# S5 branch of a hybrid encoder block: a quad's kernel emitted one quad ahead of its body

## Chip, cores and metric

One NeuronCore of a Trainium2 chip runs the whole block. The metric is the device time of one execution in microseconds, here the median of three runs. TensorE is written PE, VectorE DVE, ScalarE ACT, GpSimd POOL, SyncE (whose queue issues nearly all DMAs) SP.

## What is computed

The block normalises its input, projects it (`w_in`) and sends parts of the projection through three branches, of which S5 is one; a gated feed-forward stage follows. S5 is a bidirectional diagonal state space model on 32 groups of 16 channels. Of each direction the reference computes

```python
bb_re = coef_re[..., None] * b_re - coef_im[..., None] * b_im
bb_im = coef_re[..., None] * b_im + coef_im[..., None] * b_re
ug = u.reshape(bsz, seq, S5_GROUPS, S5_GROUP)
bu_re = jnp.einsum('blgc,gpc->lbgp', ug, bb_re)
bu_im = jnp.einsum('blgc,gpc->lbgp', ug, bb_im)
...
_, _, s_re, s_im = lax.associative_scan(combine, (a_re, a_im, bu_re, bu_im), reverse=reverse, axis=0)
y = jnp.einsum('lbgp,gcp->blgc', s_re, c_re) - jnp.einsum('lbgp,gcp->blgc', s_im, c_im)
```

and then `z = gelu(y + D*u)` and `z * sigmoid(z @ glu_w + glu_b)`. The last is called the GLU below.

## The kernel before, in words

`emit_s5` goes over eight *quads* of four groups each. Time is cut into 128 blocks of 8 steps. For one quad the program has these parts, in the order in which it emits them.

- **The kernel.** The loads of b and c (`braw`, `craw`, L780 and L781), two transposes of c on PE (`tc`, L786), the powers of the state matrix times c on DVE (`cc`, four products at L797 and two sums at L798), the product of coef and b on POOL (`bb`), and from these the local response of a block, `kp` (L819, eight matmuls), which ACT copies into `Kt` and `kb` (L823, L824) and to which DVE adds the skip term (L825, L826). `Kt` is written to DRAM as lines (L828, L829) and comes back as a Toeplitz matrix `D` by eight loads (L832).
- **Weights of the input.** `Bw` (POOL, by `cmul`), transposed on PE (`tt`, L807, two groups of four) and copied by ACT to `BT` (L809). They stand inside the kernel's code, between `bb` and `kp`. The PSUM tiles `tc`, `tt` and `kp` share one tag with two buffers.
- **The body.** The load of `U` (L835), sine and cosine of the phases (L839 to L850; DVE's share is L840, L841, four times L843, L849, L850), the products of weights and input `bu` on PE (L856, two groups of four), their rotation on DVE (L860 to L862), four scans on DVE (L868, L870), the rotation back to `M` (L875 to L877, one half on DVE, the other on POOL), the outputs `yp` on PE (L881 with `cc` and `M`, L883 with `D` and `U`), and a copy `z` by ACT (L885) that goes to DRAM.

A scheduler that simulates the engines sets the order on each engine; the order in which the program emits is one of its inputs. Each engine executes its list in that order. While S5 runs, PE also works on the projection of the remaining columns (`pj`, three lines L144 to L146 of a helper, with weights that ACT casts to `wh` at L135 and POOL subtracts to `wl` at L136). Behind the last quad come the GLU (loads `zf` at L1263, gelu and split `zh`, `zl` at L1264 to L1266, matmuls `gl`) and a branch whose fold (DVE, L299, L301, L306) runs beside the GLU.

Of the kernel before, what the change touches and what calls it, by code (L numbers as in the profile page):

```python
# [7 lines left out]
F32 = mybir.dt.float32  # L8
# [8 lines left out]
P = 128  # L17
# [422 lines left out]
def combine_odd(E, room, inv, g, ce, so, y):  # L440

    V = E.nc.vector
    for i, z in enumerate((so, ce[:, 3::-1])):
        U, W = inv("U"), inv("W")
        for m, bank in enumerate((U, W)):
            for n in range(2):
                transform(E, bank[:, n], [A5T_OFF + 512 * m + 256 * k + P * n for k in range(2)],
                          [(g[k][m][:, i],) for k in range(2)], n == 0, n == 1, True)
        for out, own, other, t in ((z[:, 0:2], U, W, T_NTAN), (z[:, 3:1:-1], W, U, T_TAN)):
            V.tensor_tensor(out=out, in0=own, in1=out, op=ALU.add)  # L450
# [133 lines left out]
def cmul(E, pool, out, a, b, shape, tag, eng=None, conj=False):  # L584

    eng = eng or E.nc.vector
    for k, op in enumerate((ALU.add, ALU.subtract) if conj else (ALU.subtract, ALU.add)):
        t = [pool.tile(shape, F32, tag=f"{tag}{i}", name=f"{tag}{i}") for i in range(2)]
        pairs = ((a[0], b[0]), (a[1], b[1])) if k == 0 else ((a[1], b[0]), (a[0], b[1]))
        for i in range(2):  # L590
            eng.tensor_tensor(out=t[i], in0=pairs[i][0], in1=pairs[i][1], op=ALU.mult)
        eng.tensor_tensor(out=out[k], in0=t[0], in1=t[1], op=op)
# [145 lines left out]
def emit_s5(E, before):  # L738


    nc, d = E.nc, E.d
    V, GP = nc.vector, nc.gpsimd
    f, b = slice(0, 64), slice(64, 128)
    with ExitStack() as ctx:
        op = ctx.enter_context(E.tc.tile_pool(name="s5k", bufs=1, reuse_waits="tile"))
        ps = ctx.enter_context(E.tc.tile_pool(name="s5_ps", bufs=1, space=PSUM, reuse_waits="tile"))
# [5 lines left out]
        with E.tc.tile_pool(name="s5p", bufs=1, reuse_waits="tile") as pp:  # L752
            coef, r8, wh, wl, ec, eb = s5_params(E, op, pp, ps)
            before()
        sp = ctx.enter_context(E.tc.tile_pool(name="s5", bufs=1, reuse_waits="tile"))
# [13 lines left out]
            GP.memset(t, 0.0)  # L769
        T = lambda tag, shape=None, bufs=1: sp.tile(shape or [P, 4, P], F32, tag=tag, name=tag, bufs=bufs)  # L770
        beside = E.dft.tile([P, 4, 4, P], F32, tag="ax", name="beside")
        for q in range(8):
            gs = slice(4 * q, 4 * q + 4)
            B4 = lambda ap, n: ap[:, gs].unsqueeze(2).to_broadcast([P, 4, n])
            braw = [T(f"braw{i}", [P, 4, 16], 2) for i in range(2)]
# [6 lines left out]
            e4 = lambda ap, n, m: ap[:, :, gs].rearrange("p t g -> p g t").unsqueeze(3).to_broadcast([P, 4, n, m])  # L782
            b4 = lambda ap, n, m: ap.unsqueeze(2).to_broadcast([P, 4, n, m])
            pt = ps.tile([P, 2, 64], F32, tag="tt", name="tc", bufs=2)
# [7 lines left out]
            CC = [T(f"cc{i}", [P, 4, 9, 16], 2) for i in range(2)]  # L792
# [5 lines left out]
                V.tensor_tensor(out=CC[k], in0=tmp[0], in1=tmp[1], op=sgn)  # L798
            Bb = [T(f"bb{i}", [P, 4, 16], 2) for i in range(2)]
            cmul(E, sp, Bb, braw, [B4(coef[0], 16), B4(coef[1], 16)], [P, 4, 16], "bt", GP)  # L800
            Bw = [T(f"bw{i}", [P, 4, 8, 16]) for i in range(2)]
            cmul(E, sp, Bw, [b4(x, 8, 16) for x in Bb], [e4(x, 8, 16) for x in eb], [P, 4, 8, 16], "wt", GP)
            BT = []
            for i in range(2):
                pt = ps.tile([P, 4, P], F32, tag="tt", name="tt", bufs=2)
                for g in range(4):
                    nc.tensor.transpose(pt[:, g], Bw[i][:, g].rearrange("p t c -> p (t c)"), E.ident)  # L807
                bt = T(f"BT{i}")
                nc.scalar.copy(bt, pt)  # L809
                BT.append(bt)  # L810
            for k in range(2):
                for s in range(2):
                    r = slice(64 * s, 64 * s + 64)
# [16 lines left out]
            D = T("D", bufs=2)  # L830
            for t in range(8):
                nc.sync.dma_start(out=D[16 * t:16 * t + 16],  # L832
                                  in_=E.klines[gs, :, 16 * (7 - t):16 * (7 - t) + P].rearrange("g c x -> c g x"))
            U = T("U", bufs=2)
            nc.sync.dma_start(out=U, in_=E.uS[gs].rearrange("g t c j -> (t c) g j"))  # L835
            J = lambda ap: ap[:, gs].unsqueeze(2).to_broadcast([P, 4, P])
# [16 lines left out]
            for i in range(2):  # L853
                pt = ps.tile([P, 4, P], F32, tag=f"bu{i}", name=f"bu{i}")
                for g in range(4):
                    nc.tensor.matmul(out=pt[:, g], lhsT=BT[i][:, g], rhs=U[:, g], start=True, stop=True)  # L856
                bu.append(pt)
            for i, sgn in ((0, ALU.add), (1, ALU.subtract)):
                p = [T(f"rt{k}") for k in range(2)]
# [5 lines left out]
            n = 4 * W  # L865
            for i in range(2):
                o, r, x = fl(S[i]), fl(rd), fl(xs[i])
# [5 lines left out]
            for i, sgn, eng in ((0, ALU.subtract, V), (1, ALU.add, GP)):  # L873
                p = [beside[:, 2 * (q % 2) + k] if i else T(f"rt{k}") for k in range(2)]
# [4 lines left out]
            for g in range(4):  # L879
                for k in range(2):  # L880
                    nc.tensor.matmul(out=yp[:, g], lhsT=CC[k][:, g, 1:9].rearrange("p i c -> p (i c)"), rhs=M[k][:, g],  # L881
                                     start=k == 0, stop=False)
                nc.tensor.matmul(out=yp[:, g], lhsT=D[:, g], rhs=U[:, g], start=False, stop=True)  # L883
            z = T("z")
# [895 lines left out]
def hybrid_block(tc, d):  # L1780
# [4 lines left out]
    with ExitStack() as top:  # L1785
# [18 lines left out]
        with ExitStack() as s0:  # L1804
            E.h0 = pool(s0, "h0")
            E.dft = pool(s1, "dft")
            with ExitStack() as s2:
# [25 lines left out]
                for ct in range(4):  # L1833
                    emit_conv(E, ct)
                emit_ada(E, (2, 4, 3), *ada_rooms(E))
                emit_s5(E, lambda: [emit_u(E, ct) for ct in range(4)])
                for ct in range(4, 12):
                    emit_conv(E, ct)
# [70 lines left out]
```

## Time and profile before

| | us |
|---|---|
| median of 3 runs (lowest, highest) | 1742.25 (1740.11, 1743.9) |
| the profiled execution | 1741.92 |
| its span | 1740.1 |
| busy in the span: PE, DVE, ACT, POOL | 1548.8, 1352.2, 720.0, 674.4 |
| S5 stretch, from the first quad's `M` to the last's | 430 to 629 |
| GLU matmuls | 674 to 701 |

The span is that of the one core; the time of an execution adds what lies around it (1.8 us here). Busy shares are averages over stages that are bound by different engines, so the S5 stretch is read by itself below. In the rows a time is the start in us from the start of the span, followed by the duration; what stands in brackets is the time that the engine idled before, and what it waited for. A matmul of f32 shows up as two rows of the trace.

### The profile page before, as it was taken

The page shows a single profiled execution, that of the slowest core. Times are in us where ns is not written, and L with a number is a line of the kernel's source. Part 1 is how long each engine was busy: PE and PEld are TensorE (multiplying, and loading weights), DVE is VectorE, ACT ScalarE, POOL GpSimd, SP SyncE. Part 2 cuts the span into 40 slices and gives each one's busy share as a digit, 9 for nine tenths or more (in the row PEclk, how much of TensorE's full clock was granted, in tenths as well). Part 3 has the DMA queues.
Part 4 walks back from the last instruction along what each step waited for, and adds up shares of the span by engine and source line. Part 5 has one row for each costly group of instructions (what it writes and reads, how often), then busy time and mean ns, then how long its engine had stood idle before and what let it go on. Part 6 is the DMA issues. An engine that isn't in the chain of part 4 may idle for free. (4 is left out here: it accounts for less than half of the span.)

```text
span 1740.1 us, 21907 instructions
## 1 busy us (share of the span) xinstructions
PE 1548.8 (89%) x7470; PEld 1282.4 (74%) x7470; DVE 1352.2 (78%) x1945; ACT 720.0 (41%) x1326; POOL 674.4 (39%) x475
## 2 busy tenths in 40 slices
PE   6777889998777798998869999899999999999996
PEld 2666768776666676786757989688888888878884
DVE  6889798688999935788887666976676777579976
ACT  5846455543333325412223355533333333245445
POOL 3356654329775526768862121111111111011242
PEclk9999999998888899999979999899999999999998
DMA  9446643423232235874326753143323223499963
GB/s 330 122 140 185 194 120 111 154 77 102 64 78 58 76 98 168 292 236 146 120 85 208 258 176 97 49 137 112 103 91 103 91 97 103 147 374 312 331 193 124
DMA packets 245318, 263.81 MB, mean 152 GB/s; under 512 B 28120, under 2 KB 169264, under 8 KB 243765
## 3 DMA queue, kind: packets, MB, share of 16 engines
q1 hardware_dynamic: 244726, 259.99, 47.0%
q0 software_dynamic: 480, 2.42, 0.4%
q8 instruction: 59, 0.97, 0.2%
q14 instruction: 53, 0.43, 0.1%
HBM read 195.00 MB, written 67.34 MB: 151 GB/s over the span
## 5 line engine op out<-in xcount | busy, mean ns | idle before, releaser
L144 PE MATMUL pj<-hT,wh 128*128 128x512 f32 x480 | 196.0, 408 | 10.0 <-ACT cva L1180 8.9
L146 PE MATMUL pj<-hT,wl 128*128 128x512 f32 x480 | 194.5, 405 | 3.5 <-POOL wl L136 3.5
L136 POOL TENSOR_TENSOR wl<-wf,wh 128x1024 fp32r<-128x1024 f32 (+1 forms) x56 | 130.5, 2330 | 157.6 <-ACT wh L135 129.8
L136 POOL TENSOR_TENSOR wl<-wg,wh 128x1024 fp32r<-128x1024 f32 x22 | 54.7, 2488 | 346.9 <-ACT wh L135 346.8
L146 PE MATMUL gu<-h2T,op 128*128 128x512 f32 x440 | 173.1, 394 | 4.3 <-DVE op L136 4.3
L144 PE MATMUL gu<-h2T,op 128*128 128x512 f32 x440 | 171.4, 394 | 2.6 <-ACT op L135 2.5
L145 PE MATMUL gu<-h2T,op 128*128 128x512 f32 x440 | 172.7, 392 | 0.0
L135 ACT CAST op<-ws 128x512 fp32r<-128x512 f32 x88 | 54.4, 621 | 181.3 <-PE gu L146 109.4
L145 PE MATMUL dn<-dop 128*128 128x512 f32 x308 | 120.1, 390 | 0.4 <-POOL dop L136 0.4
L146 PE MATMUL dn<-dop 128*128 128x512 f32 x308 | 119.9, 389 | 0.0
L144 PEld LDWEIGHTS pj<-hT,wh 128*128 128x128 f32 x480 | 94.5, 197 | 29.5 <-ACT cva L1180 9.6
L144 PE MATMUL dn<-dop 128*128 128x512 f32 x308 | 112.4, 390 | 2.9 <-ACT dop L135 2.9
L146 PEld LDWEIGHTS pj<-hT,wl 128*128 128x128 f32 x480 | 93.9, 196 | 23.1 <-POOL wl L136 4.3
L145 PE MATMUL pj<-hT,wh 128*128 128x512 f32 x256 | 104.6, 409 | 0.0
L146 PEld LDWEIGHTS gu<-h2T,op 128*128 128x128 f32 x440 | 83.6, 190 | 22.7 <-DVE op L136 5.2
L144 PEld LDWEIGHTS gu<-h2T,op 128*128 128x128 f32 x440 | 83.7, 190 | 21.3 <-ACT op L135 3.4
L145 PEld LDWEIGHTS gu<-h2T,op 128*128 128x128 f32 x440 | 83.7, 190 | 17.2
L145 PE MATMUL pj<-lT,wh 128*128 128x512 f32 x224 | 89.8, 401 | 0.0
L136 POOL TENSOR_TENSOR dop<-bf,dop 128x512 fp32r<-128x512 f32 x17 | 32.2, 1897 | 128.8 <-ACT dop L135 112.5
L1531 DVE TENSOR_TENSOR ws<-wu 128x512 f32<-128x512 f32 x22 | 24.9, 1130 | 66.2 <-DMA wu<-in_ffn_w_gu_dram 66.2
L144 PE MATMUL wop<-woh,mT 128*128 128x256 f32 x256 | 73.1, 286 | 2.3 <-DVE tmp L1406 2.1
L145 PE MATMUL wop<-wol,mT 128*128 128x256 f32 x256 | 72.5, 283 | 0.0
(458 smaller groups left out, 4503.5 us busy)
## 6 DMA issues: line engine op xcount, KB each, us to landing
bf<-in_ffn_w_down_dram SPq DMA_DIRECT2D x105, 256.0 KB
wf<-in_w_in_dram SPq DMA_DIRECT2D x36, 512.0 KB
ada<-in_ada_w_dram SPq DMA_DIRECT2D x48, 256.0 KB
wg<-in_ffn_w_gu_dram SPq DMA_DIRECT2D x22, 512.0 KB
wu<-in_ffn_w_gu_dram SPq DMA_DIRECT2D x22, 512.0 KB
adS<-S SPq DMA_DIRECT2D x44, 256.0 KB
af<-adS SPq DMA_DIRECT2D x44, 256.0 KB
adA<-a SPq DMA_DIRECT2D x33, 256.0 KB
```

The costliest lines, as they stand in the source:

```text
L135: E.nc.scalar.copy(hi, src)
L136: (lo_eng or E.nc.vector).tensor_tensor(out=lo, in0=src, in1=bc(hi), op=ALU.subtract)
L144: E.nc.tensor.matmul(out=out, lhsT=lh, rhs=rh, start=first, stop=False, skip_group_check=shared)
L145: E.nc.tensor.matmul(out=out, lhsT=lh, rhs=rl, start=False, stop=False, skip_group_check=shared)
L146: E.nc.tensor.matmul(out=out, lhsT=ll, rhs=rh, start=False, stop=last, skip_group_check=shared)
L1531: V.tensor_tensor(out=s1, in0=u1, in1=u2, op=ALU.add)
```

## The change

The kernel part becomes a function `kernel(q)` that returns `CC`, `Bb` and `D`. It is called for quad 0 ahead of the loop, and in pass q, ahead of the body of quad q, for quad q+1. `Bw` and `BT` move to the head of the body. No instruction is added or removed, no buffer changes.

```diff
--- before.py
+++ after.py
@@ -769,7 +769,8 @@
             GP.memset(t, 0.0)
         T = lambda tag, shape=None, bufs=1: sp.tile(shape or [P, 4, P], F32, tag=tag, name=tag, bufs=bufs)
         beside = E.dft.tile([P, 4, 4, P], F32, tag="ax", name="beside")
-        for q in range(8):
+        def kernel(q):
+
             gs = slice(4 * q, 4 * q + 4)
             B4 = lambda ap, n: ap[:, gs].unsqueeze(2).to_broadcast([P, 4, n])
             braw = [T(f"braw{i}", [P, 4, 16], 2) for i in range(2)]
@@ -798,16 +799,6 @@
                 V.tensor_tensor(out=CC[k], in0=tmp[0], in1=tmp[1], op=sgn)
             Bb = [T(f"bb{i}", [P, 4, 16], 2) for i in range(2)]
             cmul(E, sp, Bb, braw, [B4(coef[0], 16), B4(coef[1], 16)], [P, 4, 16], "bt", GP)
-            Bw = [T(f"bw{i}", [P, 4, 8, 16]) for i in range(2)]
-            cmul(E, sp, Bw, [b4(x, 8, 16) for x in Bb], [e4(x, 8, 16) for x in eb], [P, 4, 8, 16], "wt", GP)
-            BT = []
-            for i in range(2):
-                pt = ps.tile([P, 4, P], F32, tag="tt", name="tt", bufs=2)
-                for g in range(4):
-                    nc.tensor.transpose(pt[:, g], Bw[i][:, g].rearrange("p t c -> p (t c)"), E.ident)
-                bt = T(f"BT{i}")
-                nc.scalar.copy(bt, pt)
-                BT.append(bt)
             for k in range(2):
                 for s in range(2):
                     r = slice(64 * s, 64 * s + 64)
@@ -831,6 +822,24 @@
             for t in range(8):
                 nc.sync.dma_start(out=D[16 * t:16 * t + 16],
                                   in_=E.klines[gs, :, 16 * (7 - t):16 * (7 - t) + P].rearrange("g c x -> c g x"))
+            return CC, Bb, D
+
+        ready = kernel(0)
+        for q in range(8):
+            gs = slice(4 * q, 4 * q + 4)
+            (CC, Bb, D), ready = ready, kernel(q + 1) if q < 7 else None
+            e4 = lambda ap, n, m: ap[:, :, gs].rearrange("p t g -> p g t").unsqueeze(3).to_broadcast([P, 4, n, m])
+            b4 = lambda ap, n, m: ap.unsqueeze(2).to_broadcast([P, 4, n, m])
+            Bw = [T(f"bw{i}", [P, 4, 8, 16]) for i in range(2)]
+            cmul(E, sp, Bw, [b4(x, 8, 16) for x in Bb], [e4(x, 8, 16) for x in eb], [P, 4, 8, 16], "wt", GP)
+            BT = []
+            for i in range(2):
+                pt = ps.tile([P, 4, P], F32, tag="tt", name="tt", bufs=2)
+                for g in range(4):
+                    nc.tensor.transpose(pt[:, g], Bw[i][:, g].rearrange("p t c -> p (t c)"), E.ident)
+                bt = T(f"BT{i}")
+                nc.scalar.copy(bt, pt)
+                BT.append(bt)
             U = T("U", bufs=2)
             nc.sync.dma_start(out=U, in_=E.uS[gs].rearrange("g t c j -> (t c) g j"))
             J = lambda ap: ap[:, gs].unsqueeze(2).to_broadcast([P, 4, P])
```

The lines from L799 on move: in the kernel after, L798 is the product of `cc` (L797 before), L799 its sum, L810 is `kp`, L816 and L817 are `kb` and `Kt`, L839 is `tt`, L865 is `bu`, L869 to L871 the rotation, L877 and L879 the scans, L890 and L892 `yp`.

How the order on the engines moves, at three places. DVE from the second `cc` of quad 4 to that quad's scans, before (buffer numbers kept; the `kb` in the last row is quad 4's):

```order
L798 TENSOR_TENSOR cc_3541<-rt_3547,rt_3548 128x576
L843 SCALAR_TENSOR_TENSOR ph<-j_2291,s5keep,ph 128x128 x4
L860 TENSOR_TENSOR rt_3653<-bu_3643,cos 128x512
L861 TENSOR_TENSOR rt_3654<-bu_3648,sin 128x512
L862 TENSOR_TENSOR xs_2816<-rt_3653,rt_3654 128x4x128
L860 TENSOR_TENSOR rt_3658<-bu_3648,cos 128x512
L861 TENSOR_TENSOR rt_3659<-bu_3643,sin 128x512
L868 SCALAR_TENSOR_TENSOR S_3663<-rd,xs_2816 64x519
L870 SCALAR_TENSOR_TENSOR S_3663<-rd,xs_2816 64x519
L862 TENSOR_TENSOR xs_2817<-rt_3658,rt_3659 128x4x128
L825 SCALAR_TENSOR_TENSOR kb<-diag,dcol,kb 64x16
```

DVE now, from the `cc` of quad 5 to the scans of quad 4 (`cc_3614`, `kb` and `Kt` are quad 5's, `bu_3716` and `bu_3721` quad 4's):

```order
L799 TENSOR_TENSOR cc_3613<-rt_3615,rt_3616 128x576
L798 TENSOR_TENSOR rt_3620<-nct,ec_2486 128x576
L798 TENSOR_TENSOR rt_3621<-nct,ec_2485 128x576
L799 TENSOR_TENSOR cc_3614<-rt_3620,rt_3621 128x576
L816 SCALAR_TENSOR_TENSOR kb<-diag,dcol,kb 64x16
L817 TENSOR_TENSOR Kt<-kp,kb 64x16
L869 TENSOR_TENSOR rt_3726<-bu_3716,cos 128x512
L870 TENSOR_TENSOR rt_3727<-bu_3721,sin 128x512
L871 TENSOR_TENSOR xs_2816<-rt_3726,rt_3727 128x4x128
L869 TENSOR_TENSOR rt_3731<-bu_3721,cos 128x512
L870 TENSOR_TENSOR rt_3732<-bu_3716,sin 128x512
L877 SCALAR_TENSOR_TENSOR S_3736<-rd,xs_2816 64x519
```

Between the `cc` and the rotation there were the phases, which now stand ahead of the last `cc`; in their place stand `kb` and `Kt`, which need `kp` of the quad ahead and stood among the scans.

PE around both `bu` groups of a quad, before (`M_3495` is the quad's before it):

```order
L144 MATMUL pj<-hT_540,wh 128x512
L145 MATMUL pj<-hT_540,wh 128x512
L146 MATMUL pj<-hT_540,wl 128x512
L856 MATMUL bu_3643<-U,BT_3581 128x128 x4
L856 MATMUL bu_3648<-U,BT_3588 128x128
L881 MATMUL yp<-M_3495,cc_3366 128x128
L856 MATMUL bu_3648<-U,BT_3588 128x128 x3
L144 MATMUL pj<-hT_550,wh 128x512
L145 MATMUL pj<-hT_550,wh 128x512
```

PE now, from the last `kp` of quad 4 to the first `bu` group of quad 3 (`bu_3547`, the second, follows 19 `pj` and two `tc` later):

```order
L810 MATMUL kp<-cc_3440,bz_2815 128x144
L146 MATMUL pj<-hT_560,wl 128x512
L144 MATMUL pj<-hT_570,wh 128x512
L145 MATMUL pj<-hT_570,wh 128x512
L839 MATMUL tt<-ident,bw_3494 128x128 x4
L865 MATMUL bu_3542<-U,BT_3510 128x128 x4
L146 MATMUL pj<-hT_570,wl 128x512
```

Before, both groups of `bu` of this quad stood ahead of its `kp`; now the second `tt` and both groups stand behind all eight `kp` of the next quad. Between one quad's `M` and the next's PE had some 47 `pj` on average. It now has 103 to 106 in each of the four steps from quad 0 to 4, 60 in the next step and none in the last two.

PE behind the last `yp`, before:

```order
L881 MATMUL yp<-M_4192,cc_4063 128x128
L883 MATMUL yp<-U,D 128x128
L146 MATMUL pj<-hT_560,wl 128x512
L144 MATMUL pj<-hT_570,wh 128x512
L145 MATMUL pj<-hT_570,wh 128x512
L146 MATMUL pj<-hT_570,wl 128x512
```

PE behind the last `yp` now:

```order
L890 MATMUL yp<-M_4192,cc_3962 128x128
L892 MATMUL yp<-U,D 128x128
L144 MATMUL gl<-zh_5677,wh 128x512 x3
L145 MATMUL gl<-zl_5681,wh 128x512
L146 MATMUL gl<-zh_5677,wl 128x512
```

Of the 581 `pj` between the first `tc` and the GLU, 148 stood behind the last `yp`, and none does now. On DVE the fold (L299, L301, L306, two triples) moves from beside the GLU into the steps of quads 4 to 6, one triple each. On SP all 32 loads `zf` of the GLU now stand behind the last quad's store of `z`.

## Rows read from the trace of the kernel before

**Rows 1.** Windows: an inner quad, and the last; busy us of each engine (instructions)

```profile
548.00:576.00 28.00, 19.61 (x103) 16.20 (x102) 27.70 (x29) 9.24 (x22) 16.94 (x11) 0.83 0.18 54
601.00:629.00 28.00, 23.14 (x121) 20.12 (x121) 23.19 (x24) 3.89 (x7) 10.57 (x5) 0.94 0.36 105
```

The columns are the window and its length, then PE, PEld, DVE, ACT, POOL, the granted clock, the DMA share and GB/s.

**Rows 2.** Source line L832, the loads of D: ns min/median/max, first and last start

```profile
L832 SPq DMA_DIRECT2D D<-klines x64: 302/424/1385, 418.2 to 620.0; - x64
```

**Rows 3.** Timeline of DVE, six of the eight quads

```profile
429.26 0.69 DVE L877 TENSOR_TENSOR M<-rt,rt 128x512 f32<-128x512 f32 x1
...
458.82 0.78 DVE L850 SCALAR_TENSOR_TENSOR sin<-ph,phk 128x512 f32<-128x512 f32 x1
...
474.08 0.68 DVE L860 TENSOR_TENSOR rt<-bu,cos 128x512 f32<-128x512 f32 x1
...
480.43 1.15 DVE L825 SCALAR_TENSOR_TENSOR kb<-diag,dcol,kb 64x16 f32<-64x16 f32 x1
...
485.50 1.49 DVE L877 TENSOR_TENSOR M<-rt,rt 128x512 f32<-128x512 f32 x1
...
546.16 1.57 DVE L877 TENSOR_TENSOR M<-rt,rt 128x512 f32<-128x512 f32 x1
...
560.37 0.68 DVE L860 TENSOR_TENSOR rt<-bu,cos 128x512 f32<-128x512 f32 x1
...
613.54 0.69 DVE L861 TENSOR_TENSOR rt<-bu,sin 128x512 f32<-128x512 f32 x1 [4.24 <-PE bu L856]
...
627.20 1.64 DVE L877 TENSOR_TENSOR M<-rt,rt 128x512 f32<-128x512 f32 x1
```

**Rows 4.** Timeline of PE, and of DVE at 404.68

```profile
391.54 0.27 PE L786 MATMUL tc<-ident,craw 64*128 64x64 f32 x1
...
404.68 0.76 DVE L798 TENSOR_TENSOR cc<-rt,rt 128x576 f32<-128x576 f32 x1
...
424.26 1.05 PE L856 MATMUL bu<-U,BT 128*128 128x128 f32 x8
...
471.07 1.98 PE L819 MATMUL kp<-cc,bz 128*128 128x144 f32 x14 [0.41 <-DVE cc L798]
...
544.68 0.63 PE L807 MATMUL tt<-ident,bw 128*128 128x128 f32 x4 [1.77 <-DVE Kt L826]
...
613.26 0.47 PE L145 MATMUL pj<-hT,wh 128*128 128x512 f32 x1
...
626.06 0.39 PE L144 MATMUL pj<-hT,wh 128*128 128x512 f32 x1
```

**Rows 5.** Timeline of ACT, SP and DVE from the last z to the GLU

```profile
634.26 0.59 ACT L885 COPY z<-yp 128x512 f32<-128x512 f32 x1 [9.44 <-PE yp L883]
...
639.72 9.07 SPq L1263 DMA_DIRECT2D zf<-zS  x16
...
660.21 1.25 SPq L1263 DMA_DIRECT2D zf<-zS  x3
...
663.80 1.07 ACT L1264 ACTIVATE zf<-zf 128x1024 f32<-128x1024 f32 x1
...
666.20 2.12 ACT L1265 CAST zh<-zf 128x1024 fp32r<-128x1024 f32 x1
...
668.35 2.32 DVE L1266 TENSOR_TENSOR zl<-zf,zh 128x1024 fp32r<-128x1024 f32 x1 [2.04 <-DMA gates<-ga]
```

**Rows 6.** The GLU's tile gl: its last matmuls, and what PE waited for

```profile
L146 PE MATMUL gl<-zh,wl x32: 389/389/628, 674.4 to 700.5; 128*128 128x512 f32 x32
...
  POOL wl L136: 6.0, 2
```

**Rows 7.** Timeline of DVE beside the GLU: the first triple of the fold

```profile
677.86 1.23 DVE L299 TENSOR_TENSOR ze<-T 128x1024 f32<-128x1024 f32 x1 [7.19 <-DMA T<-vT]
...
680.26 1.79 DVE L306 TENSOR_TENSOR fq<-ze 128x512 f32<-128x512 f32 x1
```

**Rows 8.** Timeline of POOL and DVE: a scan beside a subtraction of weights

```profile
620.42 3.33 POOL L136 TENSOR_TENSOR wl<-wf,wh 128x1024 fp32r<-128x1024 f32 x1
...
621.56 3.28 DVE L870 TENSOR_TENSOR_SCAN S<-rd,xs 64x519 f32<-64x519 f32 x1
```

## Prediction before the run

> **What bounds the kernel now.** I read the table of the profile first, then windows over the S5 stretch, one for each quad, then the timelines of DVE and PE inside them, and last what each engine waited for. The windows show an inner quad with DVE busy 27.70 of 28 us and PE 19.61, and the last quad, where DVE drops to 23.19 [rows 1]. So DVE's list sets the pace of S5: its `M` products end at 429.95 for quad 0, at 547.73 for quad 4 and at 628.84 for quad 7 [rows 3], which is 117.8 us for the first four steps (29.4 each) and 81.1 us for the last three.
>
> What the change offers to remove is the way of the local kernel through DRAM. The loads of `D` are issued from 418.2 to 620.0 us at a median of 424 ns for each issue [rows 2], no engine's wait names them, and the wait of a quad's first `yp` is for DVE's `M`. I put the gain of the earlier `D` at nothing: the cover is `yp`'s place behind 12 us of DVE's scans, and it stays. What decides is the new order of the lists.
>
> **The wait that the change brings.** In DVE's new list `kb` and `Kt` of quad q+1 stand ahead of the rotation of quad q. They need all eight `kp`, which need DVE's second `cc`. On PE the second `tt` and both `bu` of quad q stand behind these `kp`, and `tt` must also wait for `Kt`, since the PSUM tag has two buffers; the trace has that wait already, 1.77 us, "<-DVE Kt" [rows 4]. Every later instruction of DVE, the four scans and `M` among them, is queued behind this wait. From the second `cc` to the start of the rotation's second product (L870 in the kernel after), along PE's list:
>
> - seven `kp`, 1.98 us [rows 4];
> - ACT's copies and DVE's `kb` and `Kt` before `tt` may start: no row times this path alone; an estimate of 1.45, a little below the 1.77 of the wait seen [rows 4], with 3 `pj` inside it;
> - `tt`, 0.63, and two groups of `bu` at 1.05 each [rows 4], 2.73 together;
> - the other 16 `pj` between the groups: 57 `pj` start from 613.26 to 626.06, 0.2286 apart [rows 4], so 3.7; two `tc` at 0.27 less overlap, 0.3.
>
> Together 10.1 us in which DVE does only about 1.9 us (`kb`, `Kt` and the first product).
>
> The rest of a step is DVE's own. **Front** (end of `M` to the first L860 product): 458.82 to 474.08 is 15.3, and 547.73 to 560.37 is 12.6 [rows 3]; I take 14.0, the middle. **Back** (first L861 product to the end of `M`): 474.76 to 486.99 is 12.2, or 11.0 without `kb` and `Kt`, of which `kb` is 1.15; and 613.54 to 628.84 is 15.3, or 14.9 without them [rows 3]. I take 12.5, below the middle. The reason is what POOL does: a scan took 3.28 us where it ran beside a subtraction of weights of 3.33 us [rows 8], and some of POOL's work will now fall into the stall. The Trainium skill, "SBUF — State Buffer", section "SBUF: two separate sides", says that the port pair which DVE and GpSimd share is locked for a whole instruction, and that a DVE operation with two SBUF inputs blocks against a GpSimd operation that reads SBUF. By that rule the back would be at its short end, 11.0, in every step, and my sum some 12 us lower (eight backs); the rows here, 12.2 and 15.3, contain both, so I keep 12.5.
>
> A step is thus 14.0 + 10.1 + 12.5 = 36.6 us. PE's own list for a step (103 `pj` at 0.2286, 23.5, and some 9.3 of `kp`, `tt`, `bu`, `tc` and `yp` at the prices above) is 32.8, so DVE and its wait stay the bound.
>
> **The sum**, against the profiled execution of 1741.92 us, which lies 0.3 below the median. The last landmark is the GLU's last matmul; I put everything behind it at no change, since only a few rows move there and PE's list of matmuls is the same.
>
> 1. *Start.* PE's first `tc` is at 391.54. From there to the second `bu` of quad 0 PE now has 97 `pj` (22.2), sixteen `kp` (4.5, two quads), eight `tt` (1.2), both `bu` (2.1) and `tc` (0.7): 30.7. It waits for the first `cc`, which ends at 405.44 [rows 4], some 5, since only 38 `pj` (8.7) lie ahead of its `kp`; and for the second about 1. That is 428.5, and with a back of 12.5 `M` of quad 0 ends at 441.0 instead of 429.95: **+11.1**.
> 2. *Quads 0 to 4.* Four steps of 36.6 are 146.4 instead of 117.8: **+28.6**.
> 3. *Quads 4 to 7.* The step from 4 to 5 has 36.6 and one triple of the fold, which now stands on DVE: 677.86 to 682.05 is 4.2 [rows 7], so 40.8. From 5 to 6 there are no `pj` behind `kp`: 14.0 + 4.2 + 4.4 + 12.5 = 35.1, where 4.4 is `kp`, the copies and one `bu` of the above. From 6 to 7 no kernel is left: 2.5 for phases and waits, and a back of 12.5, 15.0. Together 90.9 instead of 81.1: **+9.8**.
> 4. *Tail.* From the end of the last `z` (634.85) [rows 5] to the end of the GLU (700.5 and 0.39, 700.9) [rows 6] it is 66.05 now, with 148 `pj` in between. Without them the loads of `z` lead: 0.4 to the store, 32 loads at 9.07/16 = 0.567 [rows 5], 18.1; 2.3 from the end of the last load (661.46) to its gelu (663.80), then 1.07, 2.12 and 2.32 for gelu, `zh` and `zl` [rows 5]: 26.3. Behind that 87 of the 96 matmuls are left, at 0.2286 19.9, and I add 2.9 for half of the 6.0 that `gl` waits for POOL's weights [rows 6], which POOL can now prepare ahead. 49.1 against 66.05: **-17.0**. The fold's 8.4 leaves the GLU too, but DVE isn't what the GLU waits for.
>
> Sum +32.5: **1774 us**. With both short ends (12.6 and 11.0) the parts are +9.6, +17.0, +2.5 and -17.0, or 1754; with both long ends (15.3 and 14.9) and 5 less gained in the tail +13.5, +43.4, +19.6 and -12, or 1806. That is the forecast's own range.
>
> **Rivals.**
>
> *PE sets the pace, and the kernel is faster: 1736.* The change fills PE's idle time in S5 (8.4 of 28 us [rows 1]) with the 148 `pj` of the tail. If POOL's work falls into the stall and DVE's products run undisturbed, front and back shrink: the same `M` product takes 0.69 in one quad and 1.64 in another [rows 3]. The point is front plus back under 32.8 - 10.1 = 22.7 us; from there a step is PE's 32.8. Then the start is +4.3 (one wait of 1, back 11.0), the four steps 131.2, +13.4; the last three, with a front of 10.5 and a back of 9.5, 34.3, 28.6 and 12.0, -6.2; the tail -17.0. Sum -5.5. Against it: the shortest front and back in the rows, from different quads, make 23.6. The Trainium skill, "Perfetto Trace Analysis", section "Optimization Strategy", says that a kernel whose busiest engine changes between stretches may gain by interleaving them. By that rule this is the likely case, as S5 is DVE's and the tail PE's; the wait in the middle of the list is what speaks against it here. Chance 0.12.
>
> *No change, about 1742.* A step is PE's 32.8 here too, but the last three quads come out at the short ends (+2.5), and none of the 6.0 of POOL's waits [rows 6] is left in the tail (-19.9): with +4.3 and +13.4 the sum is +0.3. It asks for the same undisturbed products, only in the steps that hold `pj`. Chance 0.07.
>
> *The clock falls, 1782.* PE now idles in every front, ahead of `kp`. The granted clock was 0.83 in the inner quad with PE busy 19.61 of 28, and 0.94 in the last with 23.14 [rows 1]; both lie nearer to the chip's 2.4 GHz than to 1.2 GHz. At 0.83 PE's 10.1 become 11.4 and a step 37.9: +5.2 over four steps, and some 3 more at both ends. For it: the inner quads have the low value. Against it: PE will have more to do, not less. Chance 0.15.
>
> That the change does nothing is excluded, since the lists differ. The forecast keeps 0.61; 0.05 is left for a time above 1806.
>
> **How the numbers follow.** A measurement of this kernel tells 0.2%, 3.5 us, from no change. Faster: 0.12, same: 0.07, slower: 0.61 + 0.15 + 0.05 = 0.81. The range goes down to 1741, which leaves out the faster case and half of the even one, and up to 1806.
>
> **What would show it.** In the trace after, DVE should idle 2 to 3 us in front of `kb` (for `kp` by way of ACT) and 4 to 5 in front of the rotation's second product (for `bu`) in each of the quads 0 to 4, and its `M` products should end about 36.6 us apart; PE should idle for `cc` and not be busy all through. No `pj` behind the last `yp`; the GLU starts some 26 us behind `z` and ends near 733. Wrong would be: steps of 29 to 33 us with PE busy nearly throughout (the faster rival); `bu` ready when DVE comes to it; a start that is not later; or a tail that keeps its 66 us because the `zf` loads or the weights, not the `pj`, set it.

## The result, and the profile after

The changed kernel takes 1762.42 us (median of 4 runs, 1761.26 to 1764.74), the kernel before, on the same chip, 1742.18. The ratio is 1.0114, with a 95% interval of 1.0101 to 1.0126: slower by 20 us. The forecast was 1774 in a range from 1741 to 1806, slower with 0.81. The profiled execution took 1761.81; its span is 1760.0 against 1740.1, so 19.9 us longer.

The table of the profile, the lines of span and engines:

```profile
span 1760.0 us, 21874 instructions
...
PE 1544.3 (88%) x7470; PEld 1280.6 (73%) x7470; DVE 1328.1 (75%) x1945; ACT 721.0 (41%) x1326; POOL 646.7 (37%) x475
```

No engine has more to do (ACT is busy for 1 us longer). DVE is busy 24 us less than before and POOL 28 less, with the same instructions: they took less time, and the span grew all the same. So the question is where the engines stand idle. Windows of the kernel after: an inner step (from the end of one `M` to the next), the step before the last, and the stretch from the last `M` to the end of the GLU (columns as in [rows 1]):

```profile
512.60:546.50 33.90, 32.52 (x172) 27.13 (x172) 24.72 (x31) 11.78 (x26) 19.11 (x18) 1.00 0.34 103
...
620.60:655.10 34.50, 16.11 (x88) 15.01 (x88) 31.04 (x32) 9.05 (x20) 19.09 (x14) 0.70 0.10 25
...
669.70:714.20 44.50, 29.96 (x121) 23.72 (x122) 18.66 (x10) 22.69 (x22) 5.61 (x3) 0.80 0.37 115
```

Before, DVE was busy 27.70 of 28 us in an inner quad and PE 19.61 [rows 1]. Now DVE idles 9 us of an inner step and PE hardly any; behind it, with no `pj` left, PE idles half of a step of 34.5 us and a third of the GLU. The timeline of DVE in that inner step, after, shows the wait:

```profile
512.56 2.84 DVE L859 SCALAR_TENSOR_TENSOR sin<-ph,phk 128x512 f32<-128x512 f32 x1
515.33 1.41 DVE L798 TENSOR_TENSOR rt<-ct,ec 128x576 f32<-128x576 f32 x2
...
521.56 1.80 DVE L799 TENSOR_TENSOR cc<-rt,rt 128x576 f32<-128x576 f32 x1
526.22 0.23 DVE L816 SCALAR_TENSOR_TENSOR kb<-diag,dcol,kb 64x16 f32<-64x16 f32 x1 [2.86 <-ACT kb L815]
526.48 0.17 DVE L817 TENSOR_TENSOR Kt<-kp,kb 64x16 f32<-64x16 f32 x1
527.46 0.69 DVE L869 TENSOR_TENSOR rt<-bu,cos 128x512 f32<-128x512 f32 x1 [0.81 <-PE bu L865]
533.20 0.69 DVE L870 TENSOR_TENSOR rt<-bu,sin 128x512 f32<-128x512 f32 x1 [5.04 <-PE bu L865]
...
544.81 1.67 DVE L886 TENSOR_TENSOR M<-rt,rt 128x512 f32<-128x512 f32 x1
```

DVE waits 2.86 us for `kp` by way of ACT's `kb`, 0.81 for the first `bu` and 5.04 for the second. The timeline of PE in the same step, after, leaving out the `pj`, says why they are late:

```profile
520.52 0.41 PE L810 MATMUL kp<-cc,bz 128*128 128x144 f32 x2
520.77 0.60 PE L839 MATMUL tt<-ident,bw 128*128 128x128 f32 x4
523.41 1.98 PE L810 MATMUL kp<-cc,bz 128*128 128x144 f32 x14 [0.88 <-DVE cc L799]
525.93 0.60 PE L839 MATMUL tt<-ident,bw 128*128 128x128 f32 x4
526.36 1.06 PE L865 MATMUL bu<-U,BT 128*128 128x128 f32 x8
...
532.11 1.05 PE L865 MATMUL bu<-U,BT 128*128 128x128 f32 x8
546.53 0.49 PE L890 MATMUL yp<-M,cc 128*128 128x128 f32 x2 [0.44 <-DVE M L886]
```

From DVE's second `cc` (ends at 523.36) to the second product of the rotation (533.20) are 9.84 us, all of it PE's list. Summed over the four inner steps (443 to 581 us), the waits of DVE and of PE, after (us in total, times, longest):

```profile
DVE rt L870 <- PE bu L865: 18.1, 4, 5.0
DVE kb L816 <- ACT kb L815: 12.3, 4, 3.7
DVE rt L869 <- PE bu L865: 2.3, 4, 0.8
```

and those of PE in the same stretch:

```profile
PE yp L890 <- DVE M L886: 16.8, 4, 13.3
PE kp L810 <- DVE cc L799: 0.9, 1, 0.9
```

The three waits of DVE are 32.7 us, 8.2 a step. Of PE's 16.8 the 13.3 belong to the start. All waits of DVE in the four steps before (430 to 548 us):

```profile
DVE rt L861 <- PE bu L856: 1.4, 1, 1.4
DVE kb L825 <- ACT kb L824: 0.6, 1, 0.6
```

The steps grew by less than the waits, since DVE's own work became shorter. Windows over the four steps, after:

```profile
443.42:581.12 137.70, 130.84 (x684) 110.03 (x684) 103.11 (x117) 48.84 (x106) 81.11 (x69) 0.98 0.34 96
```

and before:

```profile
429.95:547.73 117.78, 88.71 (x437) 73.23 (x437) 114.84 (x118) 38.89 (x92) 90.30 (x69) 0.86 0.25 67
```

An account of the 19.9 us, from the ends of the `M` products and the last matmul of the GLU:

| stretch | before | after | measured | forecast |
|---|---|---|---|---|
| first `M` | 429.95 | 443.42 | +13.5 | +11.1 |
| four steps, quads 0 to 4 | 117.8 | 137.7 | +19.9 | +28.6 |
| three steps, quads 4 to 7 | 81.1 | 88.6 | +7.5 | +9.8 |
| last `M` to the end of the GLU | 72.1 | 44.5 | -27.6 | -17.0 |
| behind the GLU | 1039.2 | 1045.8 | +6.6 | 0 |

The tail of the kernel after, timelines of ACT, SP and DVE:

```profile
674.78 0.58 ACT L894 COPY z<-yp 128x512 f32<-128x512 f32 x1 [13.66 <-PE yp L892]
...
679.76 11.27 SPq L1272 DMA_DIRECT2D zf<-zS  x24
...
696.65 2.13 DVE L1275 TENSOR_TENSOR zl<-zf,zh 128x1024 fp32r<-128x1024 f32 x1 [1.45 <-ACT zh L1274]
```

and the GLU's tile `gl`, as in [rows 6]:

```profile
L146 PE MATMUL gl<-zh,wl x32: 388/389/629, 688.9 to 713.8; 128*128 128x512 f32 x32
...
  ACT zh L1274: 23.6, 4
```

The last `zl` ends 23.4 us behind `z` (the forecast had 26.3), since a load of `zf` is issued each 0.47 us and not each 0.567 as in [rows 5], and from there to the end are 15.4 us and not 22.8: 30 of the GLU's 96 matmuls had begun before the last `zl` was done, where I had put 9.

Behind the GLU the largest single piece, 3.2 us, is one wait in the inverse transform of the next branch, where DVE's products now stand in another order. The timeline of PE there, after:

```profile
911.54 2.93 PE L362 MATMUL U<-g,c32t 128*128 128x256 f32 x6 [8.04 <-DVE g L388]
```

and the same row before:

```profile
892.83 2.93 PE L362 MATMUL U<-g,c32t 128*128 128x256 f32 x6 [4.82 <-DVE g L388]
```

The rest of the 6.6 is spread over several stages and wasn't followed up; a part of it may be scatter of a single execution. The same stretch, from the end of the GLU to the end of the span, is 1036.9 to 1050.6 us long in the profiled executions of the experiments below, though no edit touches its code. An earlier end of the GLU is therefore not the same as an earlier end of the kernel.

### The profile page after: what moved, and what is told of

It is laid out like the page before. It is cut to its first block, busy times and chain, and to the rows that moved or that the text cites. A ratio compares the mean times of both kernels' runs of the same rounds, so it can differ in the third digit from the quotient of the medians.

```text
span 1760.0 us, 21874 instructions
## 1 busy us (share of the span) xinstructions
PE 1544.3 (88%) x7470; PEld 1280.6 (73%) x7470; DVE 1328.1 (75%) x1945; ACT 721.0 (41%) x1326; POOL 646.7 (37%) x475
## 5 line engine op out<-in xcount | busy, mean ns | idle before, releaser
L144 PE MATMUL pj<-hT,wh 128*128 128x512 f32 x480 | 193.7, 403 | 8.6 <-ACT cva L1189 8.0
L136 POOL TENSOR_TENSOR wl<-wf,wh 128x1024 fp32r<-128x1024 f32 (+1 forms) x56 | 124.2, 2219 | 193.2 <-ACT wh L135 141.3
L145 PE MATMUL pj<-hT,wh 128*128 128x512 f32 x256 | 102.7, 401 | 0.0
L136 POOL TENSOR_TENSOR dop<-bf,dop 128x512 fp32r<-128x512 f32 x17 | 42.6, 2510 | 120.2 <-ACT dop L135 117.2
L890 PE MATMUL yp<-M,cc 128*128 128x128 f32 x128 | 27.8, 348 | 53.7 <-DVE M L886 53.7
```

The lines of the kernel that those rows point to most:

```text
L136: (lo_eng or E.nc.vector).tensor_tensor(out=lo, in0=src, in1=bc(hi), op=ALU.subtract)
L144: E.nc.tensor.matmul(out=out, lhsT=lh, rhs=rh, start=first, stop=False, skip_group_check=shared)
L145: E.nc.tensor.matmul(out=out, lhsT=lh, rhs=rl, start=False, stop=False, skip_group_check=shared)
```

## Experiments

Theory W: the change costs time because on PE the second `tt` and `bu` stand behind all `kp` (in the changed kernel those of the next quad) while DVE's list asks for `bu` right behind `cc`. The rivals: PE's longer list by itself (P), emitting one quad ahead as such (Q), `kb`'s wait (K), contention (C).

| run | edit | us | ratio to before, 95% |
|---|---|---|---|
| e1 | only Bw and BT moved, no quad ahead | 1768.42 | 1.011 to 1.017 |
| e2 | next kernel emitted behind `bu` | 1743.28 | 0.9983 to 1.0011 |
| e3 | changed kernel, `kp` in `yp`'s PSUM buffer | 1738.59 | 0.9954 to 0.999 |
| e4 | changed kernel, `kb` and `Kt` on POOL | 1753.48 | 1.0045 to 1.0077 |
| e5 | one quad ahead, Bw and BT not moved | 1736.10 | 0.9937 to 0.9975 |
| e6 | e2 and `kb`, `Kt` on POOL | 1747.99 | 1.0013 to 1.0035 |
| e7 | e3 and `kb`, `Kt` on POOL | 1750.05 | 1.0019 to 1.0042 |
| e8 | kernel before, `kb` and `Kt` on POOL | 1749.10 | 1.0021 to 1.0042 |
| e9 | e5, quad 1's kernel behind quad 0's body | 1728.73 | 0.9898 to 0.994 |
| e10 | e5, next kernel emitted behind `bu` | 1738.25 | 0.9956 to 0.9981 |
| e11 | e5, next kernel emitted behind the rotation | 1746.30 | 0.9994 to 1.0024 |
| e12 | changed kernel, quad 1's kernel behind quad 0's body | 1753.06 | 1.0041 to 1.008 |

### The two halves of the change (e1, e5)

e1, against the changed kernel:

```diff
-        ready = kernel(0)
...
-            (CC, Bb, D), ready = ready, kernel(q + 1) if q < 7 else None
+            CC, Bb, D = kernel(q)
```

> Nothing is emitted ahead here: a quad's kernel stands directly in front of its own body, and of the change only the place of Bw and BT is left (behind kp instead of in front of it). Theory W (DVE waits for bu, which stands on PE behind all kp, the second tt and some pj; a step is DVE's front, this wait and DVE's back): the wait is here kp 2.0, 32 pj 7.3, tt 0.6, bu 2.1, tc 0.3, or 12.3, with a front of 10.5 and a back of 13.5 a step of 36 us, and a time of 1765 to 1775, slower than the kernel before. Rival P (PE's list sets the step, since PE was 96% busy in the inner steps of the changed kernel): 92 pj and the rest are 30.3 us a step, and the time is 1730 to 1740. Rival Q (it is the one quad ahead that costs): about 1742, as before.

1768.42: W. DVE's waits in the four inner steps of e1 are those of the changed kernel (its L869 is L870 there):

```profile
DVE rt L869 <- PE bu L864: 18.8, 4, 5.8
DVE kb L816 <- ACT kb L815: 15.2, 4, 4.2
```

A step takes 35.4 to 38.5 us with some 93 `pj` in it, and not the 30 us of P: PE's list is shorter than in the changed kernel (busy 126.23 of 147.84 us in the four steps, against 130.84 of 137.70), and the step longer. That speaks against P.

e5, against the changed kernel:

```diff
@@ kernel(q), behind bb and in front of kp
+            Bw = [T(f"bw{i}", [P, 4, 8, 16]) for i in range(2)]
...
+                BT.append(bt)
...
-            return CC, Bb, D
+            return CC, BT, D
...
-            (CC, Bb, D), ready = ready, kernel(q + 1) if q < 7 else None
+            (CC, BT, D), ready = ready, kernel(q + 1) if q < 7 else None
@@ body
-            Bw = [T(f"bw{i}", [P, 4, 8, 16]) for i in range(2)]
...
-                BT.append(bt)
```

> The other half of the change alone: the kernel one quad ahead, with Bw and BT left inside it, in front of kp, as before. In the lists kb and Kt stand among M's products, and between DVE's second cc and the second bu PE has seven kp, one tt and both bu, 4.6 us, with no pj between. Theory W: the wait is 4 us instead of 10, a step 29 to 31 us, and the time 1733 to 1748, within half a percent of the kernel before; the place of Bw and BT is what costs. Rival Q (one quad ahead costs as such): 1755 or more.

1736.10, faster than the kernel before by 0.25 to 0.63%: Q falls. I had expected a wait of 4 us and there is none: in the timeline of PE in e5 `bu` of the next quad runs a step ahead of its rotation, and waits for the buffer that DVE's rotation of this quad gives back:

```profile
522.34 2.54 PE L865 MATMUL bu<-U,BT 128*128 128x128 f32 x16 [2.60 <-DVE rt L870]
```

The four versions make a table. Emitting ahead is worth 6 us in either column (1742 to 1736, 1768 to 1762), and moving Bw and BT costs 26 in either row (1742 to 1768, 1736 to 1762). The loss of the change is the second half. The 6 us are what is left of larger pieces: in the profiled executions the GLU of e5 ends at 686.2, 14.7 us earlier than before (700.9), and 8.9 of these are lost behind it (1048.1 us against 1039.2). Why is open.

### Taking the wait out of the changed kernel (e2, e3, e4)

e2 emits the next kernel inside the body:

```diff
-            (CC, Bb, D), ready = ready, kernel(q + 1) if q < 7 else None
+            CC, Bb, D = ready
...
                 bu.append(pt)
+            ready = kernel(q + 1) if q < 7 else None
```

> The kernel of quad q+1 is emitted behind the bu of quad q instead of ahead of its body. In the lists both bu groups of a quad now stand a whole step ahead of the rotation that reads them, and kb and Kt stand among M's products again; 83 pj remain in an inner step, and none behind the last yp. Theory W: the wait for bu goes, a step is the larger of PE's list (28.3 us) and DVE's own work (24 to 28), and the tail stays as short as in the changed kernel: 1705 to 1725, faster than the kernel before. Rival P gives the same step. Rival C (what is lost is lost to contention of DVE with POOL or to DMA, wherever kp and bu stand): 1750 to 1765.

1743.28: 19 us are back, but I had expected at least twice that. DVE doesn't wait for `bu` any more, in its place stands another wait (four inner steps of e2):

```profile
DVE cc L799 <- PE yp L891: 14.2, 4, 6.6
```

`cc` has two buffers. A quad ahead, the one to be written is that which the `yp` of the quad before still reads, and in e2 there are up to 36 `pj` among those `yp`. And DVE's own work is 115.76 us in these four steps (441.8 to 574.6), 29 a step and not 24 to 28. Rival C's 1750 to 1765 missed too, and it does not explain the loss of the change: in the changed kernel's four steps DVE is busy 103.11 us, less than the 114.84 before.

e3 gives `kp` another buffer:

```diff
-            kp = ps.tile([P, 9, 16], F32, tag="tt", name="kp", bufs=2)
+            kp = ps.tile([P, 9, 16], F32, tag="yp", name="kp")
```

> As the changed kernel, but kp uses the PSUM buffer of yp and not one of the two buffers that tt shares with it, so that tt no longer waits for Kt. In the lists bu follows directly on kp, kb and Kt stand among M's products, some 56 pj remain in an inner step and 100 behind the last yp. Theory W: the wait for bu is kp 1.9 and bu 2.1, 4 us instead of 10, a step 28 us, the time 1722 to 1738. Rival P: PE's list is 22 us, DVE's own 24 to 26 sets the step, 1712 to 1722. Rival Q (one quad ahead costs as such): 1755 to 1765.

1738.59, just above W's range. Nothing of DVE waits for `bu`; a step is 29.5 to 32.0 us. One reason in my expectation was wrong, though: in the changed kernel `tt` does not wait for `Kt`. Its second group started at 525.93, while `Kt` was written at 526.48 (timelines above). The edit worked by what it did to the order of the lists.

e4 takes `kb` and `Kt` off DVE:

```diff
-            V.scalar_tensor_tensor(out=kb, in0=diag, scalar=dcol[:, q:q + 1], in1=kb, op0=ALU.mult, op1=ALU.add)
-            V.tensor_tensor(out=Kt[f, 0], in0=kp[f, 0], in1=kb, op=ALU.add)
+            kd = T("kd", [64, 16])
+            GP.tensor_tensor(out=kd, in0=diag, in1=dcol[:, q:q + 1].to_broadcast([64, 16]), op=ALU.mult)
+            GP.tensor_tensor(out=kb, in0=kd, in1=kb, op=ALU.add)
+            GP.tensor_tensor(out=Kt[f, 0], in0=Kt[f, 0], in1=kb, op=ALU.add)
```

> As the changed kernel, but kb and Kt are formed by POOL from the copies in SBUF, so that DVE has no instruction that waits for kp. PE's list and the place of bu stay nearly the same. Theory W: DVE then waits for bu all the longer, and the time stays within 5 us of the changed kernel, 1757 to 1767. Rival K (the wait of kb for kp, 12.3 us in four steps, is a cost by itself): 1745 to 1752.

1753.48 lies between the two. In the inner steps W holds: the four take 137.5 us (137.7 in the changed kernel), and the waits only moved to the two products of the rotation:

```profile
DVE rt L871 <- PE bu L867: 18.1, 4, 5.8
DVE rt L872 <- PE bu L867: 17.4, 4, 4.4
```

The 9 us come from elsewhere. The two profiled executions differ by 6.3 us only (e4's 1755.49 is the slowest of its nine): 3.4 of them lie in the step from quad 4 to 5 (36.1 instead of 39.5), where `kb` had waited 5.94 us, and 3.5 behind the GLU. The rest is open.

### Small instructions moved from DVE to POOL (e6, e7, e8)

The edit of e4, these lines of it, in three kernels where DVE did not wait for `kp`, or hardly (0.6 us in four steps of the kernel before): in e2 (that is e6), in e3 (e7) and in the kernel before (e8). It takes sixteen instructions off DVE's list and puts 24 on POOL's.

```diff
-            V.tensor_tensor(out=Kt[f, 0], in0=kp[f, 0], in1=kb, op=ALU.add)
...
+            GP.tensor_tensor(out=kb, in0=kd, in1=kb, op=ALU.add)
+            GP.tensor_tensor(out=Kt[f, 0], in0=Kt[f, 0], in1=kb, op=ALU.add)
```

> The kernel of quad q+1 emitted behind the bu of quad q, and kb and Kt formed by POOL. There DVE had 30 us of work in a step of 33 and waited 3.5 us for yp, whose last matmuls must have read the cc buffer that is written next; here DVE has 1.4 us less to do and some 8 pj fewer stand between the yp. If DVE's list and this wait set the step: 1728 to 1738. Rival P (PE's list, 28 us): unchanged, 1740 to 1746.

> kp in the PSUM buffer of yp, one quad ahead, and kb and Kt formed by POOL. In the lists some 45 pj stand in an inner step and 140 behind the last yp, nearly as in the kernel before. If DVE's list sets the step, 1.0 to 1.4 us less in each of eight: 1728 to 1735. Rival (the step is set by kp's wait for z, which holds yp's buffer, 7.7 us over four steps with the same PSUM buffer): 1738 to 1745.

> The kernel before with nothing but kb and Kt moved from DVE to POOL. If DVE's list is what sets the pace there (27.7 us of 28 busy), eight times 0.8 and 0.16 leave it: 1733 to 1738. Rival (the stalls of PE for cc, M and Kt set the pace): 1740 to 1744.

All three missed: 1747.99, 1750.05 and 1749.10, 5 to 11 us slower than without the edit. In e8 DVE has sixteen instructions less (fifteen in the windows below) and is busy for longer. A window of e8 from 391 us to its last `M`:

```profile
391.00:634.40 243.40, 185.56 (x925) 157.57 (x925) 226.37 (x210) 76.74 (x180) 169.16 (x152) 0.85 0.27 72
```

and the same of the kernel before:

```profile
391.00:628.90 237.90, 184.86 (x925) 153.72 (x923) 220.74 (x225) 76.12 (x178) 168.23 (x128) 0.87 0.28 76
```

So it is not the count of DVE's instructions that makes its list long: the others took longer. Why they did is open. POOL's queue now stands behind waits for ACT's `kb` (430 to 600 us of e8), and what follows there, the weights and POOL's half of `M`, runs at another time beside DVE:

```profile
POOL kb L827 <- ACT kb L824: 19.6, 2, 11.1
```

But this is not where e8's profiled execution falls behind. Its first `M` ends at 435.4 instead of 429.95 and its last at 634.3 instead of 628.8, so the seven steps between take as long as before; and 4.8 of these 5.5 us stand already at DVE's first product of `cc` (404.70 instead of 399.88), ahead of POOL's first `kb` at 416.95. That DVE's instructions grow when POOL runs beside them is what single rows suggest (see *The step* below); no run took POOL's work away alone.

### Using both (e9 to e12)

e9 changes e5 in one place, e12 does the same with the changed kernel:

```diff
-            (CC, BT, D), ready = ready, kernel(q + 1) if q < 7 else None
+            CC, BT, D = ready
+            if 0 < q < 7:
+                ready = kernel(q + 1)
...
+            if q == 0:
+                ready = kernel(1)
```

> As the version with Bw and BT left in the kernel, one quad ahead, but quad 1's kernel is emitted behind the body of quad 0, so that only one kernel stands ahead of the first M. If DVE's list sets the pace (it has the same work, in another place), the first M comes at 430 instead of 441, the step behind it is longer by as much, and the last M stays within 4 us of 630: 1731 to 1741. Rival S (the later start is a loss by itself): 1724 to 1729.

> The changed kernel, with quad 1's kernel emitted behind the body of quad 0, nothing else. In the version with Bw and BT left in the kernel the same edit was worth 7 us. If the start is a loss by itself (DVE's list ahead of the first M holds two kernels, and PE's the pj that belong behind it): the first M at 432 to 434 instead of 443.4, the last some 7 earlier than 669.7, and 1752 to 1758. If the wait for bu in the step behind it, which now follows two kernels, takes it back: 1760 to 1766.

e9 takes 1728.73 us, faster than the kernel before by 0.6 to 1.0%, the best of all. The first `M` comes at 431.1 (441.3 in e5) and the last at 622.7 (629.8): of the 10.2 us the steps take back 3.1 only, and my expectation that they take back nearly all fell. How the 7.1 reach the end is not shown, though. e9 leaves 87 `pj` behind the last `yp`, e5 32, and PE sits idle for the GLU's weights. What PE waited for ahead of the tile `gl` in e9:

```profile
  ACT wh L135: 13.6, 2
  POOL wl L136: 13.4, 4
```

So e9's GLU ends at 688.9, 2.7 us later than e5's, and its profiled execution (1733.97, the slowest of its six, against 1736.10) is ahead by what lies behind the GLU. Where the 7 us between the medians come from is open.

In e12, against the changed kernel, the last `M` ends at 662.4 instead of 669.7, the GLU at 707.8 instead of 714.2, and the time is 1753.06 instead of 1762.42; but the late start isn't shown to be the reason there either. The first `M` ends at 435.7 instead of 443.4, the four steps behind it take 146.9 us instead of 137.7, and at quad 4 e12 is 1.5 us behind. What it wins is won in the step from quad 5 to 6, 25.4 us instead of 34.5, where POOL is busy 10.28 us instead of 19.12 and DVE 22.80 instead of 31.07: there the changed kernel has rows of the fold (L307 to L326), all of which e12 has one step earlier, and that step is hardly longer for it (39.8 us, against 39.5). So the edit gains in both kernels, in e12 by the place of the fold as far as the rows show, in e9 by what is open.

Windows of e9, the four inner steps, the last three, and the tail:

```profile
431.10:555.70 124.60, 105.11 (x544) 86.56 (x544) 122.72 (x125) 43.52 (x105) 102.18 (x77) 0.92 0.28 74
555.70:622.70 67.00, 56.49 (x294) 47.70 (x294) 65.83 (x74) 21.73 (x45) 27.88 (x16) 0.91 0.31 89
622.70:688.90 66.20, 53.00 (x208) 43.06 (x209) 28.13 (x17) 31.87 (x40) 33.13 (x16) 0.85 0.47 151
```

DVE is busy to 98% in S5 with its list as long as before, and PE has 105.11 us of work beside it, where the kernel before had 88.71 in its four steps.

e10 and e11 put the next kernel at other places of e5's body, behind `bu` and behind the rotation; of e11's edit only the line that differs is shown second:

```diff
-            (CC, BT, D), ready = ready, kernel(q + 1) if q < 7 else None
+            CC, BT, D = ready
...
                 bu.append(pt)
+            ready = kernel(q + 1) if q < 7 else None
```

> Bw and BT left in the kernel, and the kernel of quad q+1 emitted behind the bu of quad q. DVE's list is that of the version that emits it ahead of the body but for one row; on PE bu follows kp at once (one row of tt between), and 90 instead of 32 pj are left behind the last yp. DVE's list as the bound: 1732 to 1742. If the pj in the tail decide: 58 times 0.2286, 13 us more, 1745 to 1750.

```diff
                 V.tensor_tensor(out=xs[i][:, :, 1:P + 1], in0=p[0], in1=p[1], op=sgn)
+            ready = kernel(q + 1) if q < 7 else None
```

> Bw and BT left in the kernel, and the kernel of quad q+1 emitted behind the rotation of quad q. In the lists bu is complete before the M of the quad before it, cc stands among the scans, and kb stands right behind the rotation; 184 pj are left behind the last yp, more than in the kernel before. DVE's list as the bound of S5 and the tail's pj as the bound behind it: no faster than the kernel before, 1740 to 1750. If what counts is that DVE never waits: 1730 to 1738.

e10: 1738.25, as expected of DVE's list. e11: 1746.30, no faster. There the last `M` is the earliest of all, at 618.3, and DVE never waits for PE, but its windows show why nothing comes of it: 184 `pj` are left for the tail, and PE is busy in 72.80 of its 79.5 us.

```profile
437.50:554.20 116.70, 83.19 (x436) 69.70 (x434) 114.48 (x118) 37.94 (x91) 83.72 (x68) 0.85 0.26 69
618.30:697.80 79.50, 72.80 (x314) 59.12 (x315) 29.40 (x16) 37.12 (x48) 38.20 (x18) 0.96 0.49 157
```

## Why the prediction was right, and where not

*No gain from the earlier D.* Right as far as it can be read: no wait in the profile after names `D` or its lines. What emitting ahead is worth came otherwise. From the kernel before to e5 `pj` move out of the tail: 32 are left there of 148, and the GLU ends 14.7 us earlier although the last `M` is 1.0 later. From e1 to the changed kernel, which both leave none there, the first `M` is 10.1 later, but the four steps are 10.1 shorter and the last three 10.4.

*The wait.* Right in place and size: 10.1 forecast, 9.96, 9.19, 9.84 and 9.60 measured from the second `cc` to the rotation's second product. Inside it the term of 1.45 for ACT's copies and `Kt` in front of `tt` was wrong: `tt` started 2.52 us behind the start of the seven `kp` (525.93 and 523.41, above), which is their 1.98 and most of the three `pj`, and waited for nothing. Without it the sum would have been 9.4. Two of the steps have 2 or 3 `pj` more than the 19 that I took, which brings it to the 9.65 of the mean.

*The step.* 36.6 was forecast, 34.4 is the mean of the four. Front 14.0 was the step that failed: 11.8, 9.5, 10.7 and 9.7 were measured, 10.4 in the mean. Back 12.5 was too short: 14.6, 14.1, 13.3 and 15.4, 14.3 in the mean. That the step came within 2.2 us is in part luck: the front's 3.6 and the back's 1.8 have opposite signs. I had put the relief from POOL in the back; it came in the front. The timeline of POOL before, in the front of the step behind quad 4:

```profile
548.94 2.69 POOL L591 TENSOR_TENSOR wt<-bb,eb 128x512 f32<-128x512 f32 x2
551.71 1.66 POOL L592 TENSOR_TENSOR bw<-wt,wt 128x512 f32<-128x512 f32 x1
553.44 3.07 POOL L591 TENSOR_TENSOR wt<-bb,eb 128x512 f32<-128x512 f32 x2
```

DVE's first two products of `cc` beside it, before:

```profile
550.59 3.39 DVE L797 TENSOR_TENSOR rt<-ct,ec 128x576 f32<-128x576 f32 x2
```

and POOL in the front of the step shown above, after:

```profile
512.08 2.78 POOL L136 TENSOR_TENSOR wl<-wf,wh 128x1024 fp32r<-128x1024 f32 x1
521.46 1.29 POOL L592 TENSOR_TENSOR bw<-wt,wt 128x512 f32<-128x512 f32 x1 [6.59 <-PE tt L839]
```

The same two products take 3.39 us beside POOL's work on `Bw` and 1.41 (at 515.33, above) where POOL waits 6.59 us for PE to read the old `bw`. The rule that the prediction weighed, of the Trainium skill, "SBUF — State Buffer", section "SBUF: two separate sides", fits these rows. It would have put the relief wherever POOL stands still, and only the order of POOL's list, which I had not read for this, says that this is the front.

*The rivals.* PE did come near to setting the pace, 32.52 us of 33.9, as the first rival had it (32.8 for its list), but its point, front plus back under 22.7, was not reached: 24.7. The clock did not fall in the inner steps (granted 1.00 in the window shown, against 0.83 before); it was 0.70 in the step from quad 5 to 6, where no `pj` were left. The rule of the Trainium skill, "Perfetto Trace Analysis", section "Optimization Strategy", on interleaving stretches with different busy engines is not refuted: e5 and e9 interleave them without the wait, at 1736.10 and 1728.73 us.

*Start, tail, rest.* +13.5 for +11.1 and -27.6 for -17.0. In the start, 391.54 is the second of two `tc`; the first stands at 389.99 before and at 391.51 after, so 1.5 us of the start lie ahead of S5. The tail was the term most off, by the two reasons given above. Of its 10.6 us 6.6 were made up for by the stretch behind the GLU, which I had put at nothing; that is luck. That the time fell into a range of 65 us says little by itself; what was right is the wait, its place and its size, and that the losses ahead of the tail outweigh what the tail gains.

## What to carry to other kernels

Before a stage is emitted a step ahead, read the list of each in-order engine for what the hoisted part is put in front of: the loss here came from the weights `Bw` and `BT`, whose transposes were taken out of the hoisted part and so came to stand on PE behind its `kp`, and `bu` with them. Work that fills another engine's gaps must be spread up to the end: `pj` that filled the inner steps were missing in the last two steps and in the GLU, and the earliest S5 (e11) gained nothing because it left 184 of them for the tail. And where a hoist is right in a loop, try its first pass by itself; the medians fell by 7 and 9 us here, though not by the way that I had expected.

## What the runs showed that was not expected

DVE's time for the same list is not a constant: 114.84 us in four steps before, 103.11 after, with the same instructions of a quad. Taking sixteen small instructions from DVE to POOL made three kernels slower by 5 to 11 us and one faster by 9, the one in which DVE waited in them for `kp`; neither was followed to its cause. And what S5 and the GLU gain or lose is not what the kernel gains or loses: the stretch behind them, whose code is the same in all runs, differed by up to 13.7 us between profiled executions.
